# Modulation products taken one by one beside attention heads, and the last eight columns taken into the expert loop

## The chip, the cores and the metric

The kernel runs on one core of a Trainium2 chip. The metric is the device time of one execution in microseconds, lower is better. All inputs start in HBM and the output ends there; the arithmetic is fp32, where a product is made of three matmuls over high and low parts of its operands.

## What is computed

Two blocks follow each other on 256 tokens of width 1024. The first is two hybrid layers (retention, sparse attention, a linear recurrent unit; then an output product and a LayerNorm). The second modulates its input by six vectors that come from a condition `c`, mixes tokens with an mLSTM and a window attention, and ends in product-key experts. Cut to what the change touches:

```python
def _adaln(cond, w, b):
    mod = jax.nn.silu(cond) @ w + b
    return tuple(m[:, None, :] for m in jnp.split(mod, 6, axis=-1))

sh1, sc1, g1, sh2, sc2, g2 = _adaln(c, w_ada, b_ada)            # w_ada: 1024 x 6144
csh1, csc1, cg1, csh2, csc2, cg2 = _adaln(c_ctx[None], w_ada, b_ada)
h_lat = _modulate(x, norm_mix_g, sh1, sc1)
h_ctx = _modulate(ctx, norm_mix_g, csh1, csc1)
y_lat, _ = _token_mixer(h_lat, h_ctx, w_in, ...)
x = x + g1 * y_lat
x = x + g2 * _peer(_modulate(x, norm_ffn_g, sh2, sc2), ...)
```

`silu(c) @ w_ada` gives 6144 numbers, 48 columns of 128. The first sixteen (`sh1`, `sc1`) are wanted for the context condition `c_ctx` too, before the second block's input products; the next eight are `g1`, wanted after the merge; then `sh2` and `sc2` before the experts; the last eight are `g2`, wanted at the very end.

## The kernel before, in words

A weight matrix of 1024 x 256 comes as two loads of 512 KB into buffers of a ring of six (`RAW`; `raw`, L189). ACT makes the high half (`whi`, L197), DVE the low half (`wlo`, L198), and PE does three matmuls for each product (L157 to L159). `load_next` issues the loads in a fixed order of names (nq0, nq1, nksw, nvsw, rgl, nkvc, lx, rq, rk, ...), ahead of their use. In each of the two layers the sparse-attention heads run token tile 1 first, then tile 0, eight heads each (from L453): three matmuls into a score tile `ps_s` (two buffers, L457 to L459), a DVE reduction `nm` (L461), two exponentials on ACT (L464), transposes on PE (`ps_pt`, L468), a copy `pT` that DVE does for four heads and ACT for the other four (L473), and the output matmuls (L476). The loads of the compression's weights (`cmpw`, L502) use the same ring of six. The window attention of the second block has the same form (from L984).

The modulation is not done on PE. `ada_steps` (L252 on) works through 24 pairs of columns. For a pair it takes two buffers of the same ring, loads two times 512 KB (`wada`, L262), and makes each column by one DVE instruction over 128 x 1024 that multiplies by the condition and sums (a dot, L265); an accumulator read follows each. The first eight pairs are also multiplied by the context's condition `cb1`, the first of the two columns in two half dots (output `junk`), since its tile must stay whole for a second reading. A table `BG` says at which weight load how many pairs are issued (`bg`, called in `load_next`); `ada_upto(4)` ahead of the context's LayerNorm (L872) and `ada_upto(12)` ahead of the experts' input take what is left by then. `gate_row` (L246) turns eight columns into a row by a PE transpose, an ACT copy and a store to DRAM, from which `g1` and `g2` are loaded broadcast over the partitions.

A scheduler decides each engine's order from this code, so the place of a dot in the code is not its place in DVE's queue; what each engine's queue is, is shown below for the places that matter. The engines' queues run in order; SP's queue holds nearly all loads, and a load whose buffer is not free holds up those behind it.

The experts end in a loop over 128 rows of `v` (`for e in range(NE - 2)`, L1489): one load of 512 KB (`eraw`), its high and low halves (`ehi` on ACT, `elo` on DVE L1270), the two halves of the row's weights (`wv`, L231 and L232), and twelve matmuls into four accumulators (L1486). `store` holds 128 rows of weights for it, so rows whose matmuls are done are free space; at e = 16 the loop reuses rows 0 to 11 for `g2` and for the residual `x3`.

Of the kernel before, what the change touches and what calls it, by code (L numbers as in the profile page):

```python
# [18 lines left out]
P = 128  # L19
T = 256  # L20
# [5 lines left out]
BG = {(0, "lx"): 1, (0, "ng0"): 1, (0, "wo2"): 1, (1, "nksw"): 2, (1, "lx"): 1, (1, "ng0"): 1, (1, "wo1"): 1,  # L26
      (1, "wo3"): 1, (2, "akvg"): 1, (3, "mq0"): 1, (3, "gm0"): 1, (3, "ga0"): 2, (3, "gm1"): 1, (3, "ga1"): 3,
      (3, "gm2"): 1, (3, "gm3"): 2, (3, "ba0"): 1, (3, "wo0"): 1, (3, "wo1"): 1}
# [54 lines left out]
def hybrid_kernel(ctx: ExitStack, tc: tile.TileContext, I, out):  # L83
# [162 lines left out]
    def gate_row(i):  # L246

        pb = pstr([8, P], "ps_gate")
        te.transpose(pb, modT[:, 24 * i + 16:24 * i + 24], ident)
        row = wk.tile([8, P], F32, name="grow", tag="t512", bufs=4)  # L250
        ac.activation(row, pb, AF.Copy)
        sy.dma_start(gdram[i].rearrange("(j p) -> j p", j=8), row)  # L252

    def ada_steps():

        for i in range(24):
# [11 lines left out]
            if i < 8:  # L268
# [5 lines left out]
                ve.tensor_tensor(m[1][:, 0:1], two[:, 0:1], two[:, 1:2], op=ALU.add)  # L274
                dot(m[0][:, 0:1], w[0], cb[0], w[0])
                dot(m[1][:, 1:2], w[1], cb[1], w[0])
            else:
                dot(m[0][:, 0:1], w[0], cb[0], w[0])
            dot(m[0][:, 1:2], w[1], cb[0], w[1])
            for v in m:  # L280
                ve.tensor_tensor(v, v, PR("bada")[:, 2 * i:2 * i + 2], op=ALU.add)
            if i == 11:
                gate_row(0)
                sy.dma_start(g1b, gdram[0:1].to_broadcast([P, D]))
            if i == 23:
                gate_row(1)
            yield

    ada_it = ada_steps()
    def bg(*at):  # L290

        for _ in range(BG.get(at, 0)):
            next(ada_it, None)
            ada_at[0] += 1

    def ada_upto(b):
        while ada_at[0] < 2 * b:
            next(ada_it)
            ada_at[0] += 1
# [91 lines left out]
    def layer(l, XT, before_out=lambda: None):  # L391
# [57 lines left out]
        for t in (1, 0):  # L449
# [3 lines left out]
            for h in (0, 4, 1, 5, 2, 6, 3, 7):  # L453
                g, j = h // 4, h % 4
# [524 lines left out]
    for t in range(2):  # L979
# [210 lines left out]
    ada_upto(12)  # L1190
# [467 lines left out]
```

## Time and profile before

| what | value |
|---|---|
| median of 3 runs | 1449.05 us (1448.88 to 1453.01) |
| profiled execution | 1449.96 us |
| its span | 1448.2 us |
| busy share of the span | PE 95%, weight loads of PE 88%, DVE 77%, ACT 49%, POOL 9% |
| chain that ended last | PE 73%, DVE 18%, DMA 3%, issue 3%, ACT 3% |
| read from HBM | 251.32 MB, 175 GB/s over the span |
| modulation loads | 48 of 512 KB, 4.4 us from issue to landing (median) |
| modulation dots on DVE | 56 whole ones, 68.0 us; 16 half ones |

The busy shares are a mean over stages. The two layers end at about 330 us, the second block's mixing at about 590 us; then come the experts' queries and selection, the products with `u` up to 1094 us, and the loop over `v` up to the end. A stretch in which PE is busy all the time can only be shortened by fewer matmuls; in the others it is read which wait ends last.

### The profile page before, as it was taken

Reading aid. Unit: us, or ns where it says so; the run is one execution under the profiler, and the core shown is the slowest. Engines: PE = TensorE matmul, PEld = TensorE weight load, DVE = VectorE, ACT = ScalarE, POOL = GpSimd, SP = SyncE. Lnnn points to the kernel's source line nnn. Section 1 sums busy time; section 2 is a strip of 40 time slices with the busy share of each in tenths; the row PEclk is TensorE's granted clock in tenths of the full one; section 3 lists DMA queues with packets and bytes.
Section 4 is the critical chain, followed back from the end, with each engine's and each line's share of the span. In section 5 each row is a group of like instructions: output and inputs, shape, how many; then the busy total and the mean of one; then the engine's idle time right before and its main releaser. Section 6 shows DMA issues by size and latency. Waiting matters only on the chain.

```text
span 1448.2 us, 26203 instructions
## 1 busy us (share of the span) xinstructions
PE 1380.5 (95%) x10136; PEld 1280.0 (88%) x10136; DVE 1111.8 (77%) x2275; ACT 704.2 (49%) x1310; POOL 132.3 (9%) x97
## 2 busy tenths in 40 slices
PE   7999889998999999899879999999999999999998
PEld 7998889898989999798779999999998888888886
DVE  7689887999888978669993488889896666666665
ACT  5654355455544544544434444444444544554553
POOL 0010001000000000016756600000000000000000
PEclk9999999999999999999999999999999999999999
DMA  8445553556447565444335544444445655555554
GB/s 307 156 153 184 166 192 118 174 190 238 160 133 229 187 229 192 146 163 143 132 131 174 176 160 147 147 160 147 154 152 190 220 195 195 191 196 195 190 195 141
DMA packets 73646, 255.13 MB, mean 176 GB/s; under 512 B 9121, under 2 KB 11569, under 8 KB 73137
## 3 DMA queue, kind: packets, MB, share of 16 engines
q1 hardware_dynamic: 72880, 251.36, 51.9%
q0 software_dynamic: 640, 2.10, 0.5%
q8 instruction: 80, 1.31, 0.4%
q14 instruction: 46, 0.37, 0.1%
HBM read 251.32 MB, written 2.11 MB: 175 GB/s over the span
## 4 chain that ended last, share of the span: by engine, by line
PE 73%; DVE 18%; DMA 3%; issue 3%; ACT 3%; SPq 0%; DVEq 0%; ACTq 0%
PE acc L1486 24%; PE ps_a L157 6%; PE ps_a L158 6%; PE ps_a L159 6%; PE ps_g L1459 3%; DVE wlo L198 3%; DMA raw<-w 2%; PE ps_o L476 1%; DVE wada L265 1%; DVE elo L1270 1%; ACT whi L197 1%; DVE rest L1288 1%; PE ps_oa L1005 1%; DVE eq L1397 1%; PE ps_num L1125 1%
## 5 line engine op out<-in xcount | busy, mean ns | idle before, releaser
L1270 DVE TENSOR_TENSOR elo<-eraw,ehi 128x1024 fp32r<-128x1024 f32 (+1 forms) x268 | 295.8, 1105 | 135.3 <-ACT ehi L1268 130.3
L1268 ACT ACTIVATE ehi<-eraw 128x1024 fp32r<-128x1024 f32 x268 | 282.1, 1053 | 194.6 <-PE ps_a L158 105.8
L159 PE MATMUL ps_a<-XBh,elo 128*128 128x256 f32 x1024 | 292.5, 286 | 15.5 <-DVE elo L1270 13.2
L157 PE MATMUL ps_a<-XBh,ehi 128*128 128x256 f32 x1024 | 296.2, 289 | 4.7 <-ACT store L1420 4.6
L158 PE MATMUL ps_a<-XBl,ehi 128*128 128x256 f32 x1024 | 290.0, 283 | 0.0
L1486 PE MATMUL acc<-ehi,wv 128*128 128x512 f32 x1024 | 274.6, 389 | 0.0
L1486 PEld LDWEIGHTS acc<-ehi,wv 128*128 128x128 f32 x1024 | 192.1, 188 | 40.1 <-ACT wv L231 0.2
L197 ACT ACTIVATE whi<-raw 128x1024 fp32r<-128x1024 f32 (+3 forms) x138 | 144.6, 1050 | 149.1 <-DMA raw<-w 21.5
L159 PEld LDWEIGHTS ps_a<-XBh,elo 128*128 128x128 f32 x1024 | 196.3, 192 | 20.5 <-DVE elo L1270 17.4
L157 PEld LDWEIGHTS ps_a<-XBh,ehi 128*128 128x128 f32 x1024 | 196.3, 192 | 5.8 <-ACT store L1420 5.7
L158 PEld LDWEIGHTS ps_a<-XBl,ehi 128*128 128x128 f32 x1024 | 196.5, 192 | 0.0
L198 DVE TENSOR_TENSOR wlo<-raw,whi 128x1024 fp32r<-128x1024 f32 (+3 forms) x138 | 166.4, 1208 | 23.7 <-ACT whi L197 22.7
L1486 PE MATMUL acc<-elo,wv 128*128 128x512 f32 x512 | 158.4, 389 | 0.0
L1272 POOL TENSOR_TENSOR elo<-eraw,ehi 128x768 fp32r<-128x768 f32 x53 | 106.5, 2013 | 341.5 <-ACT ehi L1268 335.7
L231 ACT ACTIVATE wv<-store 128x256 fp32r<-128x256 f32 x128 | 53.4, 418 | 169.3 <-PE acc L1486 169.3
L1486 PEld LDWEIGHTS acc<-elo,wv 128*128 128x128 f32 x512 | 96.1, 188 | 19.9
L232 DVE TENSOR_TENSOR wv<-store,wv 128x256 fp32r<-128x256 f32 x128 | 54.4, 425 | 68.6 <-ACT wv L231 68.6
L265 DVE SCALAR_TENSOR_TENSOR wada<-wada,cb 128x1024 f32<-128x1024 f32 x56 | 68.0, 1216 | 3.2 <-DMA wada<-wada 3.0
L1454 DVE TENSOR_TENSOR hot<-hot,slotb 128x1024 bf16<-128x1024 bf16 x96 | 63.5, 685 | 0.2
L1452 DVE TENSOR_TENSOR hot<-iob,slotb 128x1024 bf16<-128x1024 bf16 x64 | 45.4, 711 | 23.7 <-PE ps_g L1459 23.5
L1459 PE MATMUL ps_g<-hot 128*128 128x128 bf16 x768 | 55.3, 219 | 0.5 <-DVE hot L1454 0.5
L1464 ACT ACTIVATE store<-ps_g 128x300 f32<-128x300 f32 (+31 forms) x64 | 19.2, 300 | 67.7 <-DVE store L1462 67.7
(654 smaller groups left out, 2978.4 us busy)
## 6 DMA issues: line engine op xcount, KB each, us to landing
eraw<-u SPq DMA_DIRECT2D x128, 512.0 KB, 3.6
eraw<-v SPq DMA_DIRECT2D x128, 512.0 KB, 4.3
raw<-w SPq DMA_DIRECT2D x122, 512.0 KB, 4.3
wada<-wada SPq DMA_DIRECT2D x48, 512.0 KB, 4.4
eraw<-wq SPq DMA_DIRECT2D x12, 512.0 KB, 4.2
raw<-w SPq DMA_DIRECT2D x4, 560.0 KB, 5.7
raw<-w SPq DMA_DIRECT2D x4, 544.0 KB, 4.9
cmpw<-cmpw SPq DMA_DIRECT2D x4, 512.0 KB, 6.8
```

The source lines that it names most:

```text
L157: te.matmul(o, A[0], B[0], start=start, stop=False)
L158: te.matmul(o, A[0], B[1], start=False, stop=False)
L159: te.matmul(o, A[1], B[0], start=False, stop=stop)
L197: ac.activation(hi[:, m], r[:, m], AF.Copy)
L198: ve.tensor_tensor(lo[:, m], r[:, m], hi[:, m].bitcast(F32), op=ALU.subtract)
L265: ve.scalar_tensor_tensor(out, x, 0.5, c, op0=ALU.mult, op1=ALU.mult, accum_out=o)
L1268: ac.activation(hi, raw, AF.Copy)
L1270: ve.tensor_tensor(lo[:, :n], raw[:, :n], hi[:, :n].bitcast(F32), op=ALU.subtract)
L1272: po.tensor_tensor(lo[:, n:], raw[:, n:], hi[:, n:].bitcast(F32), op=ALU.subtract)
L1454: ve.tensor_tensor(hot[:, i], hot[:, 2], of(2 + i), op=ALU.mult)
L1459: te.matmul(pg[:, j, :], at(3), at(i), start=(i == 0), stop=(i == 2))
L1486: te.matmul(acc[t][h], a[:, ts_], b[:, 512 * h:512 * h + 512], start=(e == 0 and i == 0), stop=(e == NE - 1 and i == 2))
```

## The change

It moves the 48 columns in time, in three ways. (1) `ada_steps` yields after each dot (after the two half dots together), so that a pair is four steps or two. One step is placed into six of the eight heads of each token tile in both layers, and into the four heads with g = 1 in each tile of the window attention. `BG` shrinks to eight entries; its entries and `ada_upto` keep counting in pairs. (2) Only 40 columns (20 pairs) are made before the experts. (3) The last eight columns are made in the loop over `v`. At e = 32 the condition is loaded and its silu formed again, in rows 20 to 27 of `store`; at e = 36, 40, ..., 64 one column of `w_ada` is loaded into rows 24 to 31 (two places in turn) with one dot; at e = 72 the bias is added, the transpose, copy and store of `gate_row` follow, and `g2` is loaded. `x3` stays at e = 16.

The diff, cut to its core:

```diff
-BG = {(0, "lx"): 1, (0, "ng0"): 1, (0, "wo2"): 1, (1, "nksw"): 2, (1, "lx"): 1, ...
+BG = {(0, "lx"): 1, (1, "lx"): 1, (3, "gm0"): 1, (3, "ga0"): 2, (3, "gm1"): 1, (3, "ga1"): 2, (3, "gm2"): 1, (3, "ga2"): 1}
...
-        for i in range(24):
+        for i in range(20):
...
                 ve.tensor_tensor(m[1][:, 0:1], two[:, 0:1], two[:, 1:2], op=ALU.add)
+                yield
                 dot(m[0][:, 0:1], w[0], cb[0], w[0])
+                yield
                 dot(m[1][:, 1:2], w[1], cb[1], w[0])
             else:
                 dot(m[0][:, 0:1], w[0], cb[0], w[0])
+            yield
             dot(m[0][:, 1:2], w[1], cb[0], w[1])
...
-    def bg(*at):
-
-        for _ in range(BG.get(at, 0)):
+    def ada(n):
+
+        for _ in range(n):
             next(ada_it, None)
             ada_at[0] += 1
 
+    def bg(*at):
+
+        for _ in range(BG.get(at, 0)):
+            ada(4 if ada_at[0] < 32 else 2)
+
     def ada_upto(b):
-        while ada_at[0] < 2 * b:
-            next(ada_it)
-            ada_at[0] += 1
+        ada(max(0, min(8 * b, 16 + 4 * b) - ada_at[0]))
...
             for h in (0, 4, 1, 5, 2, 6, 3, 7):
+                if h not in (3, 7):
+                    ada(1)
...
             g, j = h // 4, h % 4
+            if g:
+                ada(1)
...
-    ada_upto(12)
+    ada_upto(10)
...
         if e == 16:
-
-            g2 = store[:, 0:4, :].rearrange("p a b -> p (a b)")
-            x3 = store[:, 4:12, :].rearrange("p (t a) b -> p t (a b)", t=2)
+            sy.dma_start(x3, x3dram)
+        if e == 32:
+            cnd, th = rows4(20), rows4(24)
+            sy.dma_start(cnd, ROW("c").to_broadcast([P, D]))
+            ac.activation(th, cnd, AF.Tanh, scale=0.5)
+            ve.scalar_tensor_tensor(cnd, th, 1.0, cnd, op0=ALU.add, op1=ALU.mult)
...
+        if e in range(36, 68, 4):
+            j = (e - 36) // 4
+            wa = rows4(24 + 4 * (j % 2))
+            sy.dma_start(wa, I["wada"][:, D * (40 + j):D * (41 + j)])
+            ve.scalar_tensor_tensor(wa, wa, 0.5, cnd, op0=ALU.mult, op1=ALU.mult, accum_out=m2[:, j:j + 1])
+        if e == 72:
+            ve.tensor_tensor(m2, m2, bias, op=ALU.add)
+            gate_row(1, m2, psa.tile([P, T], F32, name="ps_gate2", tag="a", bufs=2)[0:8, 0:P],
+                     gx.tile([8, P], F32, name="grow2"))
             sy.dma_start(g2, gdram[1:2].to_broadcast([P, D]))
-            sy.dma_start(x3, x3dram)
```

The order of DVE at the start of the heads of layer 0, token tile 1, before (`nm` the reductions, `pT` the copies, `wlo` a weight's low half):

```order
66 L461 TENSOR_REDUCE nm<-ps_s 128x2 x2
67 L473 COPY pT<-ps_pt 128x512 x2
68 L461 TENSOR_REDUCE nm<-ps_s 128x2 x2
69 L198 TENSOR_TENSOR wlo<-raw,whi 128x1024
70 L461 TENSOR_REDUCE nm<-ps_s 128x2
71 L198 TENSOR_TENSOR wlo<-raw,whi 128x1024
72 L461 TENSOR_REDUCE nm<-ps_s 128x2
73 L473 COPY pT<-ps_pt 128x512
74 L461 TENSOR_REDUCE nm<-ps_s 128x2
75 L473 COPY pT<-ps_pt 128x512
76 L461 TENSOR_REDUCE nm<-ps_s 128x2
77 L198 TENSOR_TENSOR wlo<-raw,whi 128x1024
```

And the order of DVE there now (`modT` and `modC` take the columns for `c` and `c_ctx`; L261, L463, L475 are the L265, L461, L473 of before):

```order
68 L463 TENSOR_REDUCE nm<-ps_s 128x2
69 L270 TENSOR_TENSOR modC<-two 128x1
70 L261 SCALAR_TENSOR_TENSOR wada,modT<-wada,cb_498 128x1024
71 L463 TENSOR_REDUCE nm<-ps_s 128x2
72 L475 COPY pT<-ps_pt 128x512
73 L261 SCALAR_TENSOR_TENSOR wada,modC<-wada,cb_503 128x1024
74 L475 COPY pT<-ps_pt 128x512
75 L463 TENSOR_REDUCE nm<-ps_s 128x2
76 L261 SCALAR_TENSOR_TENSOR wada,modT<-wada,cb_498 128x1024
77 L280 TENSOR_TENSOR modC<-modC,par 128x2
78 L463 TENSOR_REDUCE nm<-ps_s 128x2
79 L280 TENSOR_TENSOR modT<-modT,par 128x2
```

Dots stand between nearly all reductions and copies, and no low half of a weight is left in this part; in the part of token tile 0 there are two, where there were two before.

SP's order around the same heads and the loads that feed them, before (the two `raw` between `wada` and `cmpw` are the LRU weight lx) and, in the second fence, now:

```order
22 L237 DMA cb_809<-row 128x1024
23 L688 DMA xtok<-x 128x2x1024
24 L262 DMA wada<-wada 128x1024 x2
25 L189 DMA raw<-w 128x1024 x2
26 L502 DMA cmpw<-cmpw 128x1024 x2
27 L189 DMA raw<-w 128x1024
28 L444 DMA cmpp<-cmpp 128x32
```

```order
22 L490 DMA rope<-cst 128x2048
23 L258 DMA wada<-wada 128x1024 x6
24 L690 DMA xtok<-x 128x2x1024
25 L258 DMA wada<-wada 128x1024 x2
26 L444 DMA cmpp<-cmpp 128x32
27 L187 DMA raw<-w 128x1024 x2
28 L504 DMA cmpw<-cmpw 128x1024 x2
```

Two modulation loads stood ahead of lx, now eight; lx and `cmpw` share the ring of six buffers with them.

The order of DVE at the entry of layer 1, where the queries `qk` and the keys are formed, before and, in the second fence, now:

```order
295 L265 SCALAR_TENSOR_TENSOR junk,two<-wada,cb_809 128x512 x4
296 L274 TENSOR_TENSOR modC<-two 128x1
297 L265 SCALAR_TENSOR_TENSOR wada,modT<-wada,cb_804 128x1024
298 L274 TENSOR_TENSOR modC<-two 128x1
299 L265 SCALAR_TENSOR_TENSOR wada,modT<-wada,cb_804 128x1024
300 L381 SCALAR_TENSOR_TENSOR qk<-ps_nq,qk 64x512
301 L265 SCALAR_TENSOR_TENSOR wada,modC<-wada,cb_809 128x1024
302 L381 SCALAR_TENSOR_TENSOR qk<-ps_nq,qk 64x512
303 L265 SCALAR_TENSOR_TENSOR wada,modT<-wada,cb_804 128x1024
304 L281 TENSOR_TENSOR modC<-modC,par 128x2
305 L265 SCALAR_TENSOR_TENSOR wada,modC<-wada,cb_809 128x1024
306 L281 TENSOR_TENSOR modT<-modT,par 128x2
```

```order
300 L196 TENSOR_TENSOR wlo<-raw,whi 128x1024
301 L261 SCALAR_TENSOR_TENSOR junk,two<-wada,cb_503 128x512 x2
302 L270 TENSOR_TENSOR modC<-two 128x1
303 L261 SCALAR_TENSOR_TENSOR wada,modT<-wada,cb_498 128x1024
304 L381 SCALAR_TENSOR_TENSOR qk<-ps_nq,qk 64x512
305 L196 TENSOR_TENSOR wlo<-raw,whi 128x1024
306 L381 SCALAR_TENSOR_TENSOR qk<-ps_nq,qk 64x512
307 L196 TENSOR_TENSOR wlo<-raw,whi 128x1024
308 L261 SCALAR_TENSOR_TENSOR wada,modC<-wada,cb_503 128x1024
309 L261 SCALAR_TENSOR_TENSOR wada,modT<-wada,cb_498 128x1024
310 L381 SCALAR_TENSOR_TENSOR qk<-ps_nq,qk 64x512
311 L196 TENSOR_TENSOR wlo<-raw,whi 128x1024
```

Two pairs stood between the queries' splits in one piece, with one low half behind them; now one pair is spread between five low halves.

The order of DVE now in the loop over `v`, where the dots (L1517) have come forward from e = 36, 40, ..., 64 to rows 31 to 42 (L1508 is the silu of the condition, L1274 and L230 are the L1270 and L232 of before):

```order
1604 L1274 TENSOR_TENSOR elo<-eraw,ehi 128x1024
1605 L1508 SCALAR_TENSOR_TENSOR store<-store 128x1024
1606 L230 TENSOR_TENSOR wv<-store,wv 128x256
1607 L1274 TENSOR_TENSOR elo<-eraw,ehi 128x1024
1608 L230 TENSOR_TENSOR wv<-store,wv 128x256
1609 L1274 TENSOR_TENSOR elo<-eraw,ehi 128x1024
1610 L1517 SCALAR_TENSOR_TENSOR store,m_14390<-store 128x1024
1611 L230 TENSOR_TENSOR wv<-store,wv 128x256
1612 L1274 TENSOR_TENSOR elo<-eraw,ehi 128x1024
1613 L230 TENSOR_TENSOR wv<-store,wv 128x256
1614 L1274 TENSOR_TENSOR elo<-eraw,ehi 128x1024
1615 L1517 SCALAR_TENSOR_TENSOR store,m_14390<-store 128x1024
```

A dot stands behind a row's low half `elo`, ahead of the next row's `wv`.

## Rows read from the trace of the kernel before

**Rows 1.** The page, part 1: busy us (share of the span) and instructions.

```profile
PE 1380.5 (95%) x10136; PEld 1280.0 (88%) x10136; DVE 1111.8 (77%) x2275; ACT 704.2 (49%) x1310; POOL 132.3 (9%) x97
```

**Rows 2.** Windows: stretch, its length, busy us of PE, PEld, DVE, ACT, POOL, PEclk, DMA share, GB/s.

```profile
34.00:44.00 10.00, 8.81 (x67) 8.11 (x65) 7.18 (x11) 4.83 (x10) 0.00 (x0) 1.00 1.00 407
44.00:76.00 32.00, 31.99 (x267) 29.75 (x265) 20.43 (x38) 22.80 (x81) 3.14 (x5) 1.00 0.27 82
206.00:236.00 30.00, 30.00 (x249) 27.83 (x248) 18.78 (x37) 20.85 (x77) 2.16 (x3) 1.00 0.26 78
360.00:403.00 43.00, 41.38 (x325) 39.90 (x325) 34.73 (x88) 23.28 (x37) 0.00 (x0) 0.98 0.46 147
1094.00:1448.00 354.00, 349.14 (x1543) 288.71 (x1542) 214.55 (x262) 172.98 (x253) 0.00 (x0) 1.00 0.57 192
```

**Rows 3.** Waits of PE, 84 to 206 us: who waited, for whom, total, times, longest.

```profile
PE ps_xT L753 <- issue: 3.4, 1, 3.4
PE ps_nk L159 <- DVE wlo L198: 2.7, 1, 2.7
PE ps_s L457 <- DVE kk L388: 1.8, 2, 1.7
PE ps_lgate L157 <- DVE rs_t L127: 1.8, 1, 1.8
PE ps_yT L719 <- DVE ytk L686: 0.8, 1, 0.8
PE ps_rk L158 <- DVE wlo L198: 0.5, 1, 0.5
```

**Rows 4.** Waits of PE, 236 to 400 us (first two and last of the nine).

```profile
PE ps_aT L784 <- DVE xr L841: 2.3, 1, 2.3
PE ps_lgate L157 <- DVE rs_y L128: 1.9, 1, 1.9
...
PE ps_akv L157 <- ACT HLh L231: 0.4, 1, 0.4
```

**Rows 5.** Waits of PE, 452 to 600 us.

```profile
PE ps_G L1082 <- DVE modT L281: 1.8, 2, 1.4
```

**Rows 6.** Chain of waits, 177 to 206 us: start, length, what.

```profile
187.17 1.23 DVE wada L265 x2
...
190.47 1.14 DVE wada L265 x2
...
193.99 6.93 DMA raw<-w
```

**Rows 7.** Durations by form of line 265: min/median/max ns, first and last start.

```profile
L265 DVE SCALAR_TENSOR_TENSOR wada<-wada,cb x56: 1187/1217/1227, 81.0 to 556.6; 128x1024 f32<-128x1024 f32 x56
L265 DVE DVE_READ_ACCUMULATOR wada<-wada,cb x56: 70/82/90, 82.2 to 557.7; 128x1 f32 x56
L265 DVE SCALAR_TENSOR_TENSOR junk<-wada,cb x16: 679/685/1642, 78.5 to 297.4; 128x512 f32<-128x512 f32 x16
```

**Rows 8.** Groups of DVE, 44 to 76 us: busy, mean ns, idle before.

```profile
L461 DVE TENSOR_REDUCE nm<-ps_s 128x2 f32<-128x256 f32 (+1 forms) x15 | 8.1, 545 | 2.7 <-PE ps_s L459 2.6
L198 DVE TENSOR_TENSOR wlo<-raw,whi 128x1024 fp32r<-128x1024 f32 x5 | 6.1, 1224 | 2.8 <-ACT whi L197 2.8
L473 DVE COPY pT<-ps_pt 128x512 f32<-128x512 f32 (+1 forms) x8 | 4.4, 556 | 3.2 <-PE ps_pt L468 3.1
```

**Rows 9.** Timeline of DVE, v loop: start us, length us, what.

```profile
1201.41 0.43 DVE L232 TENSOR_TENSOR wv<-store,wv 128x256 fp32r<-128x256 f32 x1 [0.54 <-ACT wv L231]
1202.36 1.23 DVE L1270 TENSOR_TENSOR elo<-eraw,ehi 128x1024 fp32r<-128x1024 f32 x1 [0.53 <-ACT ehi L1268]
1204.13 0.42 DVE L232 TENSOR_TENSOR wv<-store,wv 128x256 fp32r<-128x256 f32 x1 [0.54 <-ACT wv L231]
```

**Rows 10.** Windows around two waits of layer 0.

```profile
76.00:84.00 8.00, 8.00 (x58) 8.00 (x58) 6.63 (x17) 1.89 (x3) 3.07 (x4) 0.79 0.89 296
156.00:168.00 12.00, 8.14 (x52) 7.19 (x52) 11.82 (x32) 4.54 (x5) 1.04 (x2) 0.86 0.56 174
```

More of the change, by code (lines that the diff above doesn't have):

```diff
@@ L24 @@
 ALPHA = 4.0 ** 0.25
-BG = {(0, "lx"): 1, (0, "ng0"): 1, (0, "wo2"): 1, (1, "nksw"): 2, (1, "lx"): 1, (1, "ng0"): 1, (1, "wo1"): 1,
-      (1, "wo3"): 1, (2, "akvg"): 1, (3, "mq0"): 1, (3, "gm0"): 1, (3, "ga0"): 2, (3, "gm1"): 1, (3, "ga1"): 3,
-      (3, "gm2"): 1, (3, "gm3"): 2, (3, "ba0"): 1, (3, "wo0"): 1, (3, "wo1"): 1}
+BG = {(0, "lx"): 1, (1, "lx"): 1, (3, "gm0"): 1, (3, "ga0"): 2, (3, "gm1"): 1, (3, "ga1"): 2, (3, "gm2"): 1, (3, "ga2"): 1}
 SH = 768
@@ L244, in hybrid_kernel, with gate_row @@
     cb = []
[L246 to L250, printed above, removed]
+    def gate_row(i, m, pb, row):
+        te.transpose(pb, m, ident)
         ac.activation(row, pb, AF.Copy)
@@ L282, in ada_steps @@
             if i == 11:
-                gate_row(0)
+                gate_row(0, modT[:, 16:24], pstr([8, P], "ps_gate"), wk.tile([8, P], F32, name="grow", tag="t512", bufs=4))
                 sy.dma_start(g1b, gdram[0:1].to_broadcast([P, D]))
-            if i == 23:
-                gate_row(1)
             yield
     ada_it = ada_steps()
+    def ada(n):
+        for _ in range(n):
+            next(ada_it, None)
+            ada_at[0] += 1
     def bg(*at):
         for _ in range(BG.get(at, 0)):
-            next(ada_it, None)
-            ada_at[0] += 1
+            ada(4 if ada_at[0] < 32 else 2)
     def ada_upto(b):
-        while ada_at[0] < 2 * b:
-            next(ada_it)
-            ada_at[0] += 1
+        ada(max(0, min(8 * b, 16 + 4 * b) - ada_at[0]))
     ada_at = [0]
@@ L1487, in weigh @@
                           stop=(e == NE - 1 and i == 2))
+    rows4 = lambda r: store[:, r:r + 4, :].rearrange("p a b -> p (a b)")
+    g2 = rows4(0)
+    x3 = store[:, 4:12, :].rearrange("p (t a) b -> p t (a b)", t=2)
     for e in range(NE - 2):
@@ L1493, in hybrid_kernel @@
         if e == 16:
-            g2 = store[:, 0:4, :].rearrange("p a b -> p (a b)")
-            x3 = store[:, 4:12, :].rearrange("p (t a) b -> p t (a b)", t=2)
+            sy.dma_start(x3, x3dram)
[4 more added lines that the diff above has]
+            ve.scalar_tensor_tensor(cnd, th, 1.0, cnd, op0=ALU.add, op1=ALU.mult)
+            bias = gx.tile([P, 8], F32, name="bias2")
+            m2 = gx.tile([P, 8], F32, name="m2")
+            o = PO["bada"][0]
+            sy.dma_start(bias, I["par"][:, o + 40:o + 48])
+        if e in range(36, 68, 4):
[7 more added lines that the diff above has]
+                     gx.tile([8, P], F32, name="grow2"))
             sy.dma_start(g2, gdram[1:2].to_broadcast([P, D]))
-            sy.dma_start(x3, x3dram)
     last = [(e, weights(e), load_e(I["v"][e])) for e in (NE - 2, NE - 1)]
```

## The prediction

> **What bounds the kernel now.** I read the page's busy shares first, then the time windows, then PE's waits, then the chain of waits where a wait is long. The page gives PE 1380.5 us of a 1448.2 us span [rows 1], so 67.7 us of the span are without a matmul; a change that takes no matmul away can only win out of those. The windows show that the limit changes by stretch [rows 2]. Beside the sparse-attention heads of layer 0 (44 to 76 us) PE is busy 31.99 of 32 us and DVE 20.43; beside those of layer 1 (206 to 236) PE is busy 30.00 of 30 and DVE 18.78. Those heads are PE-bound with DVE to spare, and the loop over the expert rows of v at the end is too (PE 349.14 of 354, DVE 214.55). Between them the picture turns: PE waits there for DVE. After the heads of layer 0 it waits 1.8 + 0.8 + 0.5 us on the gate, the branch output and a weight's low half; at the entry of layer 1 2.7 us for a weight's low half and 1.8 us for the keys [rows 3]. From 236 to 400 us nine waits from 2.3 down to 0.4 us add up to 8.9 us [rows 4]. Before the merge it waits 1.8 us, 1.4 at one time, for a modulation column [rows 5].
>
> The chain of waits at the entry of layer 1 shows what DVE does meanwhile: modulation dots (187.17 to 190.47 us and on) stand in the chain, and a weight load that takes 6.93 us follows behind them [rows 6]. One dot is 1.217 + 0.082 us, a half one 0.685 + 0.082 [rows 7]. So a pair of columns with a context condition costs DVE 3 x 1.30 + 2 x 0.77 + small adds = 5.6 us, one without it 2.6 us.
>
> **The change, part by part.** The sums are against the profiled execution of 1449.96 us, which lies 0.91 us above the median of the three runs.
>
> (a) *Heads of layer 0.* The order of DVE now has pairs 0, 1 and 2 between the reductions and copies of the heads: 3 x 5.6 = 16.8 us, less the two half dots ahead of the first reduction, 15.3. Three of the five low-half splits there (five are 6.1 us, so 1.22 each [rows 8]) go behind the heads: -3.7. DVE's work is 20.43 + 15.3 - 3.7 = 32.0 us in a stretch that took 32. It stood idle 11.6 us in it, most of it in waits for PE and ACT (2.7, 2.8 and 3.2 us at the three groups shown [rows 8]). If none of those waits stays, the stretch keeps its length; if all stay, it grows by 11.6. I take one third, +3.9: the first reductions and copies, the change of token tile and the last two heads have no dot to fill them. Besides, SP now has eight modulation loads (before: two) ahead of the two of the LRU weight, and these wait for buffers that pair 1's dots free, so PE's order has 18 fewer lx matmuls and 10 fewer of the compression in the heads. At 31.99/267 = 0.12 us each [rows 2] that is 3.4 us of PE work done later. Sum **+7.3** (3.4 to 15.0).
>
> (b) *Behind those heads.* Eight dots fewer stand from there to the end of layer 0 (10.4 us of DVE). The three waits named above go: **-3.1** (0 to -3.1). The 3.4 us in front of the transposes of the new x [rows 3] stays: DVE's rows of that LayerNorm tail are the same in both orders.
>
> (c) *Entry of layer 1.* The weight loads now stand ahead of the eight modulation loads, and only three dots and two half ones (before: six and four) stand between the queries' splits. Of 2.7 + 1.7 us [rows 3] I take **-3.5** (0 to -4.4); the keys still have to be formed.
>
> (d) *Heads of layer 1.* Two pairs come in, 11.2 us, one split of 1.2 goes: 18.78 + 10.0 = 28.8 us of 30. DVE was idle for 11.2; a third of that kept gives 32.5, +2.5. Eight lx matmuls more and 16 of the compression fewer is 1.0 us moved out. **+3.5** (-0.2 to 11.0).
>
> (e) *Rest of layer 1, to the merge's input.* Ten dots fewer there. Of the 8.9 us of waits [rows 4] I take **-7.0** (0 to -8.9). The largest, 2.3 us for the context's modulation, should go whole: those transposes now stand inside the output product, behind 92 of its matmuls. What is late next: six dots more (7.8 us) come up to the stretch from 360 to 403 us, where DVE has 34.73 of 43 us [rows 2], so it is nearly full at 42.5; at 0, if that cover breaks some 2 us.
>
> (f) *Before the merge.* Seven dots fewer beside the mLSTM: **-1.2** of the 1.4 us [rows 5] (0 to -1.4).
>
> (g) *v loop.* Eight dots (1.30 us) within twelve rows. From one row to the next it is 1204.13 - 1201.41 = 2.72 us, of which DVE works 1.23 + 0.43; a dot behind a split that ends at 1202.36 + 1.23 = 1203.59 would run to 1204.89, where the split of the weights (1204.13 [rows 9]) waits 0.76 us. That has two buffers and is wanted when the next row ends, a row later. On the DMA side eight loads of 512 KB in 32.6 us add 129 GB/s to 192; 321 is below the 407 seen in the busiest ten microseconds [rows 2]. **+0.5** for a late load (0 to 10.4, every dot in PE's way).
>
> Sum: 7.3 - 3.1 - 3.5 + 3.5 - 7.0 - 1.2 + 0.5 = **-3.5**: 1446.5 on the profiled execution, 1445.6 on the median. I say 1446.
>
> The sum hangs on one unknown, the share f of DVE's idle time in the two stretches of heads that stays. With 22.8 us of idle time it is -11.1 + 22.8 f: even at f = 0.49. A measurement of this kernel can tell about 0.3%, 4.35 us, from no change; that is f under 0.30 or over 0.68. My third sits close to the first.
>
> **The rivals.**
>
> *B, the heads absorb the dots.* f near 0: every wait of DVE for PE is filled by a dot, since two heads' scores are in flight and PE has matmuls of its own to go on with. For it: PE was busy 31.99 of 32 us, so DVE's waits there are waits for a busy PE [rows 2, 8]. Against: DVE's work comes to 32.0 of 32 us, with no slack. It gives 1449.96 - 11.1 = 1439.
>
> *C, the heads become a chain on DVE (slower).* A reduction that is ready stands behind a dot of 1.22 us, its exponential behind it, then transposes, copy and output; with only two score buffers PE then waits, and does not get the LRU weight to fill in. For it: at the entry of layer 1 that very order, a split behind dots, cost 2.7 us at one place [rows 3, 6]. It is slower than before from f = 0.49; at two thirds +4.1, 1454; at one +11.7, 1462. The Trainium skill, page "TensorE: Matmul & The Clock Gate", section "Architectural detail: the array is 16× 32×32, not 1× 128×128", says that VectorE's queue is a strict FIFO. By that rule no reduction passes a dot, and this case gets nothing back from reordering on the chip; rows 6 agree, where the split starts only when the dots have ended.
>
> *D, the gaps move.* The chains of small operations behind the waits in (b), (c), (e) and (f) are long in themselves, and half of the 14.8 us comes back: 1446.5 + 7.4 = 1454 at most, 1450 if a quarter does.
>
> *E, the clock.* Around the waits of layer 0 the granted clock falls: 0.79 over 76 to 84 us and 0.86 over 156 to 168 [rows 10], both levels (2.4 and 1.2 GHz) mixed; each costs 8 x 0.21 or 12 x 0.14 = 1.7 us of matmul time. Both stretches of heads are at 1.00 today [rows 2]. If PE idles in them, one such fall per token tile is 4 x 1.7 = 6.7 us: 1453. Fewer waits later would give some of it back. The same page, section "HAM oscillation — how this bites in real kernels", says that waits between bursts of matmuls throw the engine back to the slower clock again and again; by that rule the change makes such places in the heads and removes them behind.
>
> **How the numbers follow.** My forecast 0.40, split by the bound of f into 0.18 faster and 0.22 within; B 0.22, faster; C 0.20, slower; D 0.12, 0.07 within and 0.05 slower; E 0.06, within. Together: faster 0.40, within 0.3% 0.35, slower 0.25. The cases of both signs are strong, so the likeliest one's own range is 1443 to 1449. The range runs from 1438, just under B's 1439, to 1456, over C at two thirds, D and E; C beyond f = 0.75 and worse late loads are left out, about 0.15.
>
> **What would show it.** Right: the heads of layer 0 end near 80 us with PE busy some 28.6 us of 36 and DVE over 85%; the wait of the nk product for its low half is under 1 us; lgate, yT and aT are gone from PE's waits; the v loop keeps its length within 1 us, with the eight dots in rows 31 to 42. B shows as heads of 32 us. C shows as scores that wait for DVE and heads over 40 us; D as the same wait totals under other names; E as a clock under 0.95 in the heads. I am wrong in substance if the heads cost under 3 us for both layers together or over 20, or if the v loop grows by over 2 us.

## The result, and the profile after

The changed kernel takes **1467.35 us** (median of 4 runs, 1462.98 to 1470.04) beside 1449.09 us for the kernel before: 1.0132 of its time, 95% interval 1.0101 to 1.0163. It is slower by 18 us, outside the range of the prediction. The profiled execution is the fastest of the four, 1462.98 us at a mean granted clock of 0.985; the other three ran at 0.979 to 0.985. The ledger below is of that execution and so shows 13 of the 18 us.

The page of the changed kernel, its first part:

```profile
span 1461.0 us, 26186 instructions
...
PE 1387.2 (95%) x10136; PEld 1284.6 (88%) x10136; DVE 1114.5 (76%) x2273; ACT 704.1 (48%) x1311; POOL 132.8 (9%) x97
```

Against [rows 1] the span has grown by 12.8 us. PE's busy time has grown by 6.7 us with the same 10136 matmuls, and the time without a matmul by 6.1 (from 67.7 to 73.8). So half of the loss in this execution is not waiting at all: the same matmuls took longer. Busy time could also grow because matmuls overlap less, but the clock is enough for it: laid over the trace's record of the granted clock, 35.9 us of matmul time stand at the lower of the two levels (1.2 instead of 2.4 GHz) and 23.0 us before; at half the clock the 12.9 us between them cost 6.5, an estimate. The windows (columns as in [rows 2]; the last three are granted clock, DMA share and GB/s) show where the clock has gone down:

```profile
44.00:76.00 32.00, 28.54 (x212) 25.03 (x210) 28.77 (x65) 18.46 (x70) 2.94 (x4) 0.95 0.37 120
206.00:236.00 30.00, 29.47 (x230) 25.69 (x228) 24.32 (x51) 16.62 (x61) 1.28 (x1) 1.00 0.20 61
236.00:288.00 52.00, 43.33 (x299) 38.98 (x298) 41.62 (x91) 23.44 (x46) 3.80 (x5) 0.90 0.59 192
452.00:482.00 30.00, 26.42 (x203) 25.38 (x201) 21.56 (x37) 12.33 (x21) 0.00 (x0) 0.94 0.74 239
1094.00:1461.00 367.00, 360.56 (x1646) 299.24 (x1644) 229.80 (x292) 179.74 (x268) 0.00 (x0) 1.00 0.59 202
```

In the heads of layer 0 (44 to 76 us) PE starts 212 matmuls where it started 267 [rows 2], and the clock is 0.95 instead of 1.00; DVE is busy 28.77 of 32 us. Behind the heads of layer 1 (236 to 288) the clock is 0.90. PE's waits in the two layers:

```profile
PE ps_rk L156 <- DVE wlo L196: 6.2, 2, 3.8
PE ps_pt L470 <- ACT pp L466: 4.6, 3, 1.7
PE ps_xT L755 <- issue: 3.4, 1, 3.4
PE ps_wo L155 <- ACT yTh L229: 2.3, 2, 1.1
PE ps_cs L539 <- DVE kc L230: 1.8, 1, 1.8
...
PE ps_rq L155 <- ACT xp L572: 1.5, 1, 1.5
```

The waits of [rows 3] and [rows 4] on lgate, nk, aT and the keys are gone, as forecast. In their place stand 6.2 us for the low half of rk (2.4 in layer 0 and 3.8 in layer 1; 0.5 and 1.0 before), 1.8 and 1.5 us behind the heads of layer 1 for the compression's scores (`ps_cs`) and for rq, and 4.6 us in the heads for the exponentials. Behind the window attention and in the loop over v (first fence 380 to 480 us, second 1094 us to the end):

```profile
PE ps_G L1086 <- DVE G L1077: 3.6, 1, 3.6
```

```profile
PE acc L1490 <- DVE wv L230: 1.5, 1, 1.5
```

How far the changed kernel's trace lies behind the one before, at the end of the last matmul of a tile (us in each trace):

| place (tile) | before | after | behind by | step since the place above | forecast |
|---|---|---|---|---|---|
| entry, ps_nvsw of layer 0 | 34.05 | 32.43 | -1.6 | | |
| layer 0, ps_lx (behind the heads) | 82.19 | 86.96 | 4.8 | +6.4 | (a) +7.3 |
| layer 0, ps_wo | 158.81 | 167.29 | 8.5 | +3.7 | (b) -3.1 |
| layer 1, ps_nk | 198.65 | 203.66 | 5.0 | -3.5 | (c) -3.5 |
| layer 1, ps_cs (behind heads and compression) | 248.06 | 260.03 | 12.0 | +7.0 | (d) +3.5 |
| second block, ps_akv | 366.93 | 371.63 | 4.7 | -7.3 | (e) -7.0 |
| merge, ps_wo | 581.47 | 592.31 | 10.8 | +6.1 | (f) -1.2 |
| experts, ps_a | 1094.82 | 1105.61 | 10.8 | 0.0 | 0 |
| loop over v, acc | 1443.14 | 1456.07 | 12.9 | +2.1 | (g) +0.5 |

Three steps came out within a microsecond, (a), (c) and (e); (b), (d) and (f) did not, and they lie at or right behind the three groups of heads. What each step is made of is told by windows between the same ends. These are (b) and (e), each before and after:

```profile
82.19:158.81 76.62, 72.62 (x564) 68.12 (x563) 71.80 (x181) 35.59 (x47) 0.50 (x1) 1.00 0.53 174
86.96:167.29 80.33, 76.02 (x565) 71.87 (x563) 64.40 (x154) 36.17 (x48) 0.54 (x2) 0.94 0.48 157
248.06:366.93 118.87, 109.69 (x820) 103.12 (x819) 109.21 (x269) 62.25 (x103) 1.58 (x4) 0.96 0.55 185
260.03:371.63 111.60, 104.76 (x818) 99.62 (x817) 97.94 (x236) 60.81 (x102) 1.67 (x4) 0.97 0.52 167
```

For all steps (us; the windows' length less PE's busy time is the time without a matmul):

| step | time without a matmul | matmul time | granted clock |
|---|---|---|---|
| (a) | 1.2 to 5.2 (+4.0) | +2.4 | 0.96 to 0.96 |
| (b) | 4.0 to 4.3 (+0.3) | +3.4 | 1.00 to 0.94 |
| (c) | 6.6 to 3.5 (-3.1) | -0.4 | 0.96 to 0.95 |
| (d) | 2.1 to 5.7 (+3.6) | +3.4 | 1.00 to 0.97 |
| (e) | 9.2 to 6.8 (-2.3) | -4.9 | 0.96 to 0.97 |
| (f) | 4.2 to 8.3 (+4.1) | +2.1 | 1.00 to 0.99 |
| (g) | 0.0 to 1.5 (+1.5) | +0.6 | 1.00 to 1.00 |

Each pair has the same matmuls but for two at most, so a change of matmul time is not a change of work.

### The profile page after: what moved, and what is told of

It reads as the page before. It is cut to its first block, busy times and chain, and to the rows that moved or that the text cites. A ratio compares the mean times of both kernels' runs of the same rounds, so it can differ in the third digit from the quotient of the medians.

```text
span 1461.0 us, 26186 instructions
## 1 busy us (share of the span) xinstructions
PE 1387.2 (95%) x10136; PEld 1284.6 (88%) x10136; DVE 1114.5 (76%) x2273; ACT 704.1 (48%) x1311; POOL 132.8 (9%) x97
## 4 chain that ended last, share of the span: by engine, by line
PE 77%; DVE 13%; DMA 4%; issue 3%; ACT 2%; SPq 0%; DVEq 0%; ACTq 0%
PE acc L1490 22%; PE ps_a L155 7%; PE ps_a L156 6%; PE ps_a L157 6%; PE ps_g L1463 3%; DVE elo L1274 2%; DVE wlo L196 2%; PE ps_wo L155 1%; PE ps_wo L157 1%; PE ps_wo L156 1%; PE ps_o L478 1%; DMA wada<-wada 1%; DMA store<-wada 1%; DVE rest L1292 1%; PE ps_oa L1009 1%
## 5 line engine op out<-in xcount | busy, mean ns | idle before, releaser
L1274 DVE TENSOR_TENSOR elo<-eraw,ehi 128x1024 fp32r<-128x1024 f32 (+1 forms) x268 | 300.0, 1120 | 130.6 <-ACT ehi L1272 121.4
L230 DVE TENSOR_TENSOR wv<-store,wv 128x256 fp32r<-128x256 f32 x128 | 54.2, 424 | 59.5 <-ACT wv L229 59.4
L1458 DVE TENSOR_TENSOR hot<-hot,slotb 128x1024 bf16<-128x1024 bf16 x96 | 63.5, 684 | 0.2
L261 DVE SCALAR_TENSOR_TENSOR wada<-wada,cb 128x1024 f32<-128x1024 f32 x48 | 58.2, 1214 | 4.9 <-DMA wada<-wada 4.9
```

Source lines behind the costliest of these rows:

```text
L261: ve.scalar_tensor_tensor(out, x, 0.5, c, op0=ALU.mult, op1=ALU.mult, accum_out=o)
L1274: ve.tensor_tensor(lo[:, :n], raw[:, :n], hi[:, :n].bitcast(F32), op=ALU.subtract)
L1458: ve.tensor_tensor(hot[:, i], hot[:, 2], of(2 + i), op=ALU.mult)
```

## What is late behind the heads

SP's timeline, kernel before (the two `raw` are the loads of lx), and in the second fence the changed kernel:

```profile
29.33 2.76 SPq L262 DMA_DIRECT2D wada<-wada  x2
34.63 2.76 SPq L189 DMA_DIRECT2D raw<-w  x2
38.20 1.47 SPq L502 DMA_DIRECT2D cmpw<-cmpw  x2
...
51.17 0.33 SPq L189 DMA_DIRECT2D raw<-w  x1
```

```profile
27.71 10.62 SPq L258 DMA_DIRECT2D wada<-wada  x6
...
46.09 3.36 SPq L258 DMA_DIRECT2D wada<-wada  x2
...
57.12 3.31 SPq L187 DMA_DIRECT2D raw<-w  x2
69.22 2.34 SPq L504 DMA_DIRECT2D cmpw<-cmpw  x2
73.23 36.45 SPq L187 DMA_DIRECT2D raw<-w  x13
```

The loads of lx are issued at 57.1 us instead of 34.6, those of the compression's weights at 69.2 instead of 38.2: they stand behind eight modulation loads whose buffers come free only as the dots do. The first load of the weights behind them (rq, rk and on) goes from 51.2 to 73.2 us. In layer 0 of the kernel before, 33 of lx's 48 matmuls and 20 of the compression's 32 stand between those of the heads; now 15 and none do, and the rest comes after. The chain of waits behind the heads of layer 1 shows the same with the next weights:

```profile
238.80 5.86 DMA raw<-w
...
251.51 5.01 DMA raw<-w
...
262.67 1.15 DVE wlo L196
263.86 0.58 PE ps_rk L156
```

Two weight loads of 5.9 and 5.0 us are the longest pieces of the chain, then comes the low half for rk.

## The experiments

Two theories stood against each other at first: that the loss is where the trace above drifts (little in the layers, most from the window attention to the merge), and that the dots beside the heads of the layers are the larger part of it. Each ratio is to the kernel before on the same chip. Three kernels take the change apart, and a fourth takes its loads away.

**The last eight columns alone** (the `BG` of before without its last four pairs, no dots beside heads; edit against the changed kernel):

```diff
-                if h not in (3, 7):
-                    ada(1)
...
-            if g:
-                ada(1)
```

> The kernel before with only the last eight columns moved into the loop over v; the other twenty pairs stand where they stood. Ledger theory (the loss lies where the two profiled traces drift apart: about 3 us in the two layers, 9.5 us from the window attention to the merge, 2 us in the loop over v): 1450 to 1452 us, the loop's 2 us less what the merge gains from four pairs fewer. Rival (the burst of eight dots and loads in the loop is the main loss, and the profiled run shows too little of it): 1458 us or more.

Measured: 1452.72 us, 1.0034 of the kernel before (1.0020 to 1.0047). Neither number quite; the loop has a price, nearer the first.

**Without the layers' heads** (against the changed kernel):

```diff
+BG = {(0, "lx"): 1, (0, "ng0"): 1, (0, "wo2"): 1, (1, "nksw"): 2, (1, "lx"): 1, (1, "ng0"): 1, (1, "wo1"): 1, ...
...
-                if h not in (3, 7):
-                    ada(1)
```

> The changed kernel without the dots beside the heads of the two layers; these eight pairs stand at the weight loads where they stood before. Ledger theory (window attention and merge are the larger part): about 1459 to 1461 us. Rival (the dots beside the layers' heads, and the late weight loads behind them, are the larger part): 1450 to 1453 us.

Measured: 1449.98 us, 1.0023 (1.0005 to 1.0040).

**The layers' heads alone**, all else as before (against the kernel before):

```diff
+BG = {(0, "lx"): 1, (1, "lx"): 1, (1, "wo3"): 1, (2, "akvg"): 1, (3, "mq0"): 1, (3, "gm0"): 1, (3, "ga0"): 2, ...
...
             for h in (0, 4, 1, 5, 2, 6, 3, 7):
+                if h not in (3, 7):
+                    ada(1)
```

> The kernel before with the dots beside the heads of the two layers only; the window attention, the merge and the loop over v are as before. Ledger theory: 1451 to 1453 us. Rival (the layers' heads are the larger part): 1460 to 1464 us.

Measured: 1462.17 us, 1.0095 (1.0074 to 1.0117). The rival was right both times: of 18 us the layers' heads are 14. My reading of the ledger was wrong because it put one part's gain on another's account. In the trace of no_layer_heads the window attention's part gains 9.0 us from the end of ps_wo of layer 1 to the first score (from 4.7 to 13.7 us ahead of the kernel before) and gives 9.3 back by the first ps_G. In the changed kernel the same gain hid what the layers had lost. The page of layer_heads_only says what kind of loss it is:

```profile
span 1461.4 us, 26191 instructions
...
PE 1396.3 (96%) x10136; PEld 1295.9 (89%) x10136; DVE 1114.6 (76%) x2275; ACT 703.3 (48%) x1310; POOL 134.7 (9%) x97
```

The span is 13.2 us above the kernel before and PE's busy time 15.8 us [rows 1]. PE waits less than before (65.1 us without a matmul for 67.7); by this ledger all of the loss is matmul time, at the same 10136 matmuls. The clock is enough for it: 63.5 us of matmul time stand at the lower level, 23.0 before, which by the same estimate costs 20 us. The windows from the end of `ps_nvsw` to the end of the heads of layer 0, and from the end of the nk product to the end of the heads of layer 1, have it at 0.86 and 0.92:

```profile
32.56:80.71 48.15, 44.24 (x305) 40.22 (x304) 38.69 (x83) 24.13 (x85) 3.78 (x6) 0.86 0.53 181
208.26:250.66 42.40, 40.04 (x287) 35.77 (x287) 31.99 (x70) 23.35 (x81) 2.91 (x4) 0.92 0.37 119
```

In the kernel before both are at 1.00.

**Dots without loads** (against the changed kernel):

```diff
-            w = [RAW([P, D], "wada") for _ in range(2)]
-            for a in range(2):
+            w = [RAW([P, D], "wada") for _ in range(2)] if i >= 8 else [cb[0], cb[0]]
+            for a in range(2 if i >= 8 else 0):
...
-            dot(m[0][:, 1:2], w[1], cb[0], w[1])
+            dot(m[0][:, 1:2], w[1], cb[0], w[1] if i >= 8 else g1b)
```

> The changed kernel, but the first eight pairs load nothing and hold no buffer of the ring: their dots run over a resident tile (so those sixteen modulation columns are left out of the computation and are the bias alone), and DVE's instructions stay as many and as long. If the ring and the loads are what delays the weights in the two layers: lx back in the heads, no wait for the low half of rk, 1460 us or less. If DVE's in-order queue is what costs: the same waits, within 3 us of the changed kernel's 1467.

Measured: 1462.52 us, between the two numbers. It decides nothing: with no load to wait for, the scheduler placed the dots and the weights' halves in another order (a wait of 5.4 us on the branch output of layer 0, 0.8 before), so it is not the changed kernel with its loads taken away.

**The load of lx ahead of the heads**, in layer_heads_only:

```diff
         onsa = {}
+        load_next()
 
         for t in (1, 0):
```

> layer_heads_only with the load of the LRU weight issued ahead of the heads instead of behind them, so that its matmuls can again stand between those of the heads. Clock theory: PE has its filling work back in the heads of tile 0, the clock stays up there, 1450 to 1456 us. Queue theory: the dots delay the heads all the same, 1459 to 1463.

Measured: 1449.80 us, 1.0015 (0.9997 to 1.0034). One line takes 12 of the 14 us away. It moves lx's splits and the pair of columns that `BG` ties to lx along with the load, so the run tells what the place of lx costs, not the load by itself. SP's timeline now:

```profile
29.05 2.76 SPq L261 DMA_DIRECT2D wada<-wada  x2
34.34 2.76 SPq L188 DMA_DIRECT2D raw<-w  x2
37.92 11.80 SPq L261 DMA_DIRECT2D wada<-wada  x6
...
55.43 2.07 SPq L510 DMA_DIRECT2D cmpw<-cmpw  x2
```

The heads of layer 0 do not get shorter by it: they end at 90.11 us (80.71 in layer_heads_only). But by then all 48 matmuls of lx, all 32 of the compression and 12 of rq's are done; by the end of `ps_wo` of layer 0 lx_first is 4.7 us behind the kernel before, layer_heads_only 12.6.

**Useless matmuls in the heads.** The same kernel without that line, but with four matmuls more per head:

```diff
                 pt = pstr([P, 2, nk, P], "ps_pt")
+                for _ in range(4):
+                    te.matmul(pt[:, :, 0, :], identb, bc(nleb, 2, 1), start=True, stop=True)
```

> layer_heads_only (1462 us) with four matmuls of 256 columns more per head, written where the transposes of the same head overwrite them: 128 of them, about 0.12 us each, 15 us of PE work that nothing needs. Clock theory: with PE kept at work in the heads its clock is not lowered there, and the 15 us are mostly paid for: 1455 to 1465 us, and the stretch from 60 to 100 us near a granted clock of 1.00. Queue theory (heads wait for dots in DVE's order, PE's pace is not the limit): the work fits in the waits or adds to them, 1462 to 1477, with the clock as low as without.

Measured: 1464.90 us, 1.0107 (1.0073 to 1.0141), 2.7 us above layer_heads_only. That lies in both ranges of the expectation, so the time alone does not decide. The control, the same 128 matmuls in the kernel before:

> The kernel before with the same 128 useless matmuls (15 us of PE work) beside the heads of the two layers as in filler. If those heads are bound by PE, as the windows of the kernel before say (31.99 of 32 us, clock 1.00), nearly all of it is added: 1458 to 1463 us. If PE has room there even before, or the matmuls are cheaper than 0.12 us: under 1453.

Measured: 1460.71 us, 1.0077 (1.0053 to 1.0101), 12.2 us above its kernel before (1448.48). So the same work costs 12 us in the heads of before and 3 us in the heads with dots; with the intervals of the three ratios the 9 us between them are uncertain by 7. The windows 44 to 76 and 60 to 100 us of layer_heads_only, then of filler, then of lx_first:

```profile
44.00:76.00 32.00, 29.27 (x204) 26.00 (x203) 27.66 (x62) 17.93 (x67) 2.19 (x3) 0.84 0.35 106
60.00:100.00 40.00, 36.69 (x231) 34.69 (x230) 30.09 (x77) 17.01 (x52) 6.16 (x8) 0.74 0.51 173
```

```profile
44.00:76.00 32.00, 31.86 (x260) 28.06 (x260) 26.52 (x61) 16.96 (x65) 1.58 (x1) 1.00 0.37 115
60.00:100.00 40.00, 38.03 (x294) 35.83 (x294) 29.85 (x75) 18.22 (x56) 6.46 (x8) 0.91 0.54 182
```

```profile
44.00:76.00 32.00, 29.32 (x223) 25.51 (x222) 29.73 (x68) 14.92 (x52) 1.57 (x1) 1.00 0.50 166
60.00:100.00 40.00, 35.68 (x261) 31.14 (x260) 33.77 (x82) 20.72 (x68) 6.43 (x8) 0.96 0.49 153
```

With nothing to fill PE's pauses the clock is 0.84 and 0.74. With useless work it is 1.00 and 0.91, with lx in time 1.00 and 0.96. A part of the useless work went into PE's pauses (busy 31.86 instead of 29.27 of 32 us), so its low price is not the clock's doing alone. The first windows of layer_heads_only and lx_first have nearly the same busy time, but 204 matmuls stand in the one and 223 in the other. Behind the heads of layer 1 filler's clock is low again (0.83 over 240 to 280 us, layer_heads_only 0.79, lx_first 0.96); the useless matmuls stand in the heads alone and bring no weight sooner.

**The loop over v, spread:**

```diff
-            wa = rows4(24 + 4 * (j % 2))
+            wa = rows4(e - 4)
```

> Only the last eight columns in the loop over v, as in v_only, but each column's load goes into the four rows of store that have just been used, so that it cannot start before its row is reached: eight dots over 32 rows instead of 12. Theory (the burst of loads makes dots wait for their data at the head of DVE's queue): PE's two waits of 1.3 and 0.7 us in the loop go, about 1448 to 1450 us, 3 us under v_only. Rival (a dot delays the next row wherever it stands): 1452 to 1453 as v_only.

Measured: 1447.43 us beside 1447.40, 1.0002 (0.9979 to 1.0025): PE has no wait in the loop any more. In the changed kernel the chain of waits there is:

```profile
1197.51 6.94 DMA store<-wada
...
1204.52 1.11 issue
...
1205.71 0.35 DVE wv L230
```

A modulation load takes 6.94 us among the others, the dot stands at the head of DVE's queue until it lands, and the row's `wv` behind it is late by 1.5 us. My bound had DVE's time and the transfer rate right and left out that a dot waits for its own load.

**The window attention alone**, four pairs moved beside its heads (against the kernel before):

```diff
-      (1, "wo3"): 1, (2, "akvg"): 1, (3, "mq0"): 1, (3, "gm0"): 1, (3, "ga0"): 2, (3, "gm1"): 1, (3, "ga1"): 3,
+      (3, "gm0"): 1, (3, "ga0"): 2, (3, "gm1"): 1, (3, "ga1"): 2, ...
...
+            if g:
+                ada(1)
```

> The kernel before, with four pairs moved from the end of layer 1 and the start of the second block to beside the heads of the window attention; layers, merge and loop over v as before. Clock theory (in the two layers' heads the slower TensorE clock is the loss; the window attention keeps PE busy, so dots beside it cost nothing): the 5 to 8 us that the profile of the kernel without layer heads gains there stay, and nothing is lost in the loop over v: 1441 to 1445 us beside 1448. Rival (dots beside any heads cost): 1449 or more.

Measured: 1452.17 us, 1.0018 (0.9999 to 1.0037), no gain, though its trace is 9.5 us ahead of the kernel before at the window attention's first score; by the first `ps_G` 0.4 us of that are left. **The two mends in the whole change** (lx_first and v_spread), and **the same without the window attention's dots:**

> The changed kernel with both faults mended that the runs so far point to: the LRU weight's load ahead of the heads, and each of the last eight columns' loads held to its own four rows of store. If these two are all of the loss (12 us and 3 to 5 us of 18): 1449 to 1453 us beside 1447. If the dots beside the heads cost something of their own: 1455 or more.

Measured: 1455.79 us, 1.0041 (1.0024 to 1.0059).

> As fixed_all, but without the dots beside the window attention's heads; their pairs stand at the loads of the kernel before. If the dots beside the window attention give back behind it what they gain ahead of it: the same as fixed_all within 3 us, 1446 to 1451. If they cost 4 us, as the run of that part alone has it (1452 beside 1447): 1444 to 1448, the fastest so far.

Measured: 1451.15 us, 1.0015 (1.0000 to 1.0030). So the two mends are not all; some 4 us hang on the window attention. The same line ahead of its heads:

```diff
     at = act.tile([P, 2, 512], F32, name="at", tag="hs")
+    load_next()
     for t in range(2):
```

> a_heads_only (1452 us) with the next weight's load issued ahead of the window attention's heads, as lx_first does in the layers. If it is the same mechanism (modulation loads ahead of a weight in the ring take PE's filling work away): 1445 to 1448. If something else costs there, as the modulation columns that are late behind the heads (the wait of the G transposes was 2.7 us, 1.4 before): 1450 to 1453 as without.

Measured: 1445.94 us, **0.9977** (0.9962 to 0.9992), faster than the kernel before and 0.4% below the same kernel without the line. The window from 452 to 482 us of a_heads_only and, in the second fence, of a_first:

```profile
452.00:482.00 30.00, 27.12 (x197) 26.09 (x196) 23.95 (x35) 10.75 (x17) 0.00 (x0) 0.89 0.72 225
```

```profile
452.00:482.00 30.00, 28.90 (x223) 26.52 (x222) 29.31 (x56) 15.86 (x36) 0.00 (x0) 1.00 0.77 249
```

DVE 29.31 of 30 us instead of 23.95, the clock 1.00 instead of 0.89. DVE was not too busy there in a_heads_only, but stood waiting. The changed kernel's DVE shows for what:

```profile
464.98 1.23 DVE L261 SCALAR_TENSOR_TENSOR wada<-wada,cb 128x1024 f32<-128x1024 f32 x1 [2.12 <-DMA wada<-wada]
...
472.23 1.23 DVE L261 SCALAR_TENSOR_TENSOR wada<-wada,cb 128x1024 f32<-128x1024 f32 x1 [1.93 <-DMA wada<-wada]
...
473.99 1.21 DVE L1072 TENSOR_TENSOR_SCAN F<-cmx,rows 8x512 f32<-8x512 f32 x1
475.12 1.19 DVE L261 SCALAR_TENSOR_TENSOR wada<-wada,cb 128x1024 f32<-128x1024 f32 x1
```

Two dots wait 2.12 and 1.93 us for their own loads, and the scan F for the mLSTM's gates stands behind the second. A third dot runs between F and G. That is the wait of G, 3.6 us. In a_heads_only it is 2.7 us; in a_first no dot of DVE from 395 to 475 us waits for its load any more, and what is left in front of G is 0.7 us, for a column:

```profile
PE ps_G L1091 <- DVE modT L284: 1.1, 2, 0.7
```

**Half the dots in the layers**, on top of fixed_no_a:

```diff
-                if h not in (3, 7):
+                if h in (0, 1, 2):
                     ada(1)
```

> As fixed_no_a (1451 beside 1448), with a dot beside three heads of a token tile instead of six, so that three pairs stand there instead of six; the two pairs at the entry of layer 1 are gone as in the change. If each dot in the heads costs by itself (about 0.1 to 0.2 us): 1446 to 1449, the half of the cost with the whole gain at the entry. If the number of dots there doesn't matter once lx is in time: 1450 to 1452.

Measured: 1445.34 us, 0.9979 (0.9963 to 0.9995). Against fixed_no_a (1.0015) that is 0.36%, 5 us for twelve steps fewer beside the heads; the pairs taken out stand elsewhere, so this is not the price of twelve dots alone, but it is more than I had put on them.

**All of it together** (half_heads with the window attention's dots and the load ahead of them):

> The change's idea with all four mends: in the layers a dot beside three heads of a token tile with lx loaded first, beside the window attention four heads of a tile with the next weight loaded first, the last eight columns over 32 rows of v. a_first gained 0.23% and half_heads 0.21%, in different stretches: if the two gains add, 1441 to 1443 us beside 1448.5. If what each gains is the same time (the merge's columns that come earlier), 1445 to 1447.

Measured: **1443.75 us, 0.9958** (0.9943 to 0.9974) of the kernel before, 5.8 us faster. The gains add nearly whole (0.23% and 0.21% alone, 0.42% together). Not run was fixed_all with the load ahead of the window attention, so what the rest of the dots beside the layers' heads cost there stays open. Its heads of layers 0 and 1:

```profile
44.00:76.00 32.00, 31.88 (x261) 29.60 (x260) 28.10 (x60) 20.11 (x67) 1.28 (x1) 1.00 0.51 166
206.00:236.00 30.00, 30.00 (x248) 27.90 (x247) 22.51 (x50) 20.80 (x76) 2.35 (x3) 1.00 0.32 93
```

PE is as full as in the kernel before [rows 2], at a clock of 1.00, and DVE does 8 and 4 us more beside it. That is what the change set out to do. Its page, for the execution of 1440.03 us with a span of 1438.2:

```profile
PE 1375.8 (96%) x10136; PEld 1278.7 (89%) x10136; DVE 1113.4 (77%) x2273; ACT 704.9 (49%) x1311; POOL 131.4 (9%) x97
```

## Why the prediction was wrong, step by step

- **(a), the heads of layer 0: right in size** (+6.4 of +7.3), and right in kind: the heads' last output matmul ends at 78.18 us instead of 77.51, so they take 2.3 us more with the entry's 1.6 counted, and lx's displaced matmuls add 4.1.
- **(b) and (d): this is the step that failed.** I counted the displaced weights as 3.4 us of PE work "done later", let the waits behind the heads close, since DVE had fewer dots there, and put the time of the matmuls themselves as unchanged. I had read that lx waits behind eight modulation loads, and did not follow the queue on: the loads of the compression, rq and rk stand behind lx. Those came late. In (b) the wait for rk's low half (2.4 us) took the place of the waits that closed, 4.3 us without a matmul for 4.0, and the same matmuls took 3.4 us longer at a clock of 0.94 for 1.00. In (d) the heads came out as forecast (+2.2 of +2.5); behind them PE waited 1.5 us for rq and 1.8 for the compression's scores, and matmul time grew by 3.4 over the whole step. That the late weights are the cause is shown by lx_first, where 12 of 14 us come back with lx moved ahead; how the loss divides between the waits and the clock is read from one trace.
- **The clock, rival E: the right mechanism at a chance of 0.06, and at nothing in the sum.** I priced it as one fall per token tile in heads with idle time, 6.7 us. Matmul time did grow by 6.7 us in the changed kernel's profile, but that is luck: it is a sum of steps from -4.9 to +3.4, most of them behind the heads, and by the sign I had named (under 0.95 in the heads) E did not show there (0.95 and 1.00). In layer_heads_only the lower level costs more than the whole loss (15.8 us of busy time), and the larger part of it lies in the heads: 0.86 and 0.92 there, and from the heads to the next layer's entry and to `ps_akv` 0.93 and 0.95, where the kernel before has 0.97 and 0.96. The windows of filler show that the clock goes with what PE does in the heads (0.84 to 1.00); what exactly makes it fall was not tried. The rule I named there, in the Trainium skill's page "TensorE: Matmul & The Clock Gate", section "HAM oscillation — how this bites in real kernels", gives the sign: waits between bursts throw the engine back each time. These traces agree in part: 0.74 over 60 to 100 us where the weights come late and 0.96 with lx in time, but 0.84 already in the heads, where PE is busy 29.27 of 32 us and its longest wait is 1.7 us, for an exponential and not for a load.
- **Rival C: right in sign, not in mechanism.** The heads did not become a chain on DVE: the wait for exponentials in the heads is 4.6 us, and the heads of both layers together ran 4 to 5 us longer (in layer 1 they end at 244.53 us, 7.2 behind, and began 5.0 behind). Dots beside heads may have a price (half_heads), but it is the smaller part. In [rows 6] I read a split behind dots; the split is there in the same view (`191.68 1.14 DVE wlo L198`), but the longest piece is the load of 6.93 us, which starts right behind the last of these dots. A weight's load held up by dots, the mechanism of the loss, stood in that row.
- **(c): right** (-3.5), and in kind: time without a matmul went from 6.6 to 3.5 us, as read from [rows 3].
- **(e): right in number (-7.3), in part by luck.** The waits on lgate and aT of [rows 4] are gone, but the 3.8 us for rk's low half fall into this step, so time without a matmul shrank by 2.3 us and not by 7.0. The other 4.9 us are matmul time, which the forecast had at nothing; in part the clock (9.8 us of this step's matmul time stood at the lower level before, 2.9 after). In combined's trace the steps (c) and (e) are -2.3 and -8.7.
- **(f): failed like (b).** I let a wait close and named no load that is moved past the weights of the mLSTM. Eight modulation loads among the window attention's heads delay those weights and the next columns: 4.1 us more without a matmul where I had 1.2 less, and 2.1 of matmul time. a_first puts it right with one load, in the kernel that has this part alone.
- **(g): mis-sized**, 2.1 us for 0.5 in the profile, just over the 2 us that I had named as a sign of being wrong in substance, and about 5 in the runs of v_only. Both lie in the bounds I gave (0 to 10.4), and the cause is the dot's own load.
- **The range.** The bounds of (a) and (d), 15 and 11 us, held. Those of (b) and (f) ended at 0 on the upper side, and both came out above it (+3.7 and +6.1): neither a wait of another name nor the clock was let in there. So the range up to 1456 left out a kernel in which nothing closes behind the heads.
- **The premise.** That only the 67.7 us without a matmul can be won is not so, nor that a stretch in which PE is always busy is shortened by fewer matmuls alone: matmul time moves with the clock. In the changed kernel it grew by 6.7 us; in combined's profile it shrank by 4.7 of the 10.0 us by which the span did.

## What to carry to other kernels

When work with its own loads is moved beside a stretch that lives on filling work, follow the loads first: which weight's load now stands behind them in the ring, and what PE does until it lands. An operation in an in-order queue that waits for its own transfer costs more than its duration; hold such transfers to a pace, and issue the next weight ahead of them. Where PE pauses, price the matmuls around the pause at both clock levels, from rows of the same kernel.

## What was not expected of the hardware

Runs of one kernel on one chip differ by 12 us, and the clock with them: the kernel before took 1441.72 us at a mean granted clock of 0.993 and 1454.11 us at 0.986. So one profiled execution is one draw of several: the ratios of v_only and no_layer_heads differ by 0.1%, while the spans of their profiled executions (1452.7 and 1445.3 us) are 7 us apart. Which part of the change costs was only told by taking the parts one by one. What exactly in PE's stream makes the clock fall stays open.
